# Padding the rows and pools of an encoder-block kernel so that its 512-column matmul operands start at one byte residue

## The chip, the cores and the metric

The kernel runs on one NeuronCore of one Trainium2 chip. The metric is the device time of one execution in microseconds (us), and the number shown for a kernel is the median of its runs. The core has a matrix engine, TensorE (PE in the profile; its weight loads are listed apart as PEld), three engines for element-wise work (VectorE or DVE, ScalarE or ACT, GpSimd or POOL), a queue on SyncE (SP) that issues nearly all DMA transfers, and an on-chip memory, SBUF, of 128 partitions. A tile occupies the same byte addresses in each partition. In this text "the residue" of an operand is its first byte address within a partition modulo 256.

## The reference, cut to what matters

One layer of a hybrid encoder, on 16 learned tokens followed by 1024 rows of `x`, each of 1024 float32 values:

```
u = rms_norm(h) ;  z = u @ w_in                # 1024 -> 7680 columns
A: two-directional retention of 4 heads (128-row chunks), group norm, * silu(gate), @ w_ret_branch
B: attention in a window of +-128 rows, 8 heads in 2 groups, rotary, sink, * silu(gate), @ w_attn_branch
mix = sigmoid(g_A) * A + sigmoid(g_B) * B
out = h + rms_norm(mix @ w_out)                # without the first 16 rows
```

## The kernel before, in words

**Three matmuls for one.** Each float32 product is made from operands split into a high part of type float32r and a low part (the remainder). `mm3` (lines 93 to 98) issues three matmuls into the same PSUM bank: high by high (L95), low by high (L96), high by low (L97). The first argument is stationary (the weights, 128 columns, loaded into the array ahead of the matmul), the second is moving (read column by column, 512 columns in most of the kernel, 256 in the rest).

**Seven products for eight.** The gates, the query projection and the three last projections are computed as 2x2 blocks with seven block products and sums (`Phase`, lines 984 to 1160; `PROD`, line 969). A product is `for k in range(4): mm3(...)`, that is twelve matmuls of 512 columns, on one of seven moving operands: `B11`, `B21`, `T1`, `B22` are parts of `big`; `T2`, `T3`, `T4` are sums of blocks with tiles of their own.

**The moving operands.** `big` (line 153) is four tiles, high and low, of 4 rows of T = 1040 float32 values each, 4160 bytes a row. At first it holds the transposed x (`xh`, `xl`); later phases write the gated results, then `w_out`'s input, into the same tiles. A half of a row starts at column 16 or at column 528 (`half`, line 833). T2 to T4 have rows of 512 values (2048 bytes).

**Where they lie.** Pools are taken from the left end of SBUF upwards or, with `side="right"`, from the right end downwards, each as long as its tiles need. `keep` is the first on the left. In before, the first half-row of `big` starts at byte 6816, residue 160. As 4160 is 16 x 256 + 64, the next rows have residues 224, 32 and 96, and each half-row pair has the same one, since 528 columns are 2112 bytes, 8 x 256 + 64, and 16 columns are 64 bytes. The first phase's T2, T3, T4 (tiles `T2q`, `T3q`, `T4q`, right side) start at 163808, 147424 and 131040: residue 224 in every row. The later T2 to T4 (pool `yt`, left side, above `yp` and `gp`) start at 122720: residue 96 in every row. All weights of 512-column matmuls lie on the right (`wp`, later `lp`) and have residue 224, row by row.

**Stages, in order of time.** (1) Projections of q, k, v of the retention, and the retention (256-column and 512-column matmuls mixed). (2) The keys and values of the attention. (3) The first phase, `first_phase` with names ending in y: two retention gate units and the queries (bank `by`). (4) The attention, with parts of the gate products (`pe`) put between its matmuls. (5) Phase z: the remaining gates (`bz`). (6) Phases r and a: the two branch projections (`br`, `ba`). (7) Phase o: the output (`bo`). Phases 5 to 7 run as one chain of products (`run`, line 1272). The instruction order of each engine comes from a simulated schedule by priorities, made when the program is built.

**Rings.** `stage` (line 978) gives out raw tiles for the next phase's moving operands from two rings: `sg0` in pool `lp` and `sg1` in pool `yp`; each of the four blocks of an operand takes four tiles. `refill` (line 1188) loads them, forms the sums on DVE and splits them into `big` and T2 to T4 as each of those is read for the last time. `gtile` (line 981) gives out tiles of the ring `g`, for gate values (`v`, `tg`), products and scratch. `staged` and `gates_` hold the ring lengths.

```
def stage(name, j=0, dt=F32):
    return (yp if j else lp).tile([P, 512], dt, tag=f"sg{int(j)}", bufs=staged[bool(j)], name=name)
```

Of the kernel before, what the change touches and what calls it, by code (L numbers as in the profile page):

```python
# [7 lines left out]
F32 = mybir.dt.float32  # L8
R = mybir.dt.float32r
# [6 lines left out]
T = NM + SEQ  # L16
P = 128
# [39 lines left out]
def block_kernel(ctx: ExitStack, tc: tile.TileContext, xT, x, meta, w_in, w_rb, w_ab, w_out, vecs, dec, sink,  # L57
# [4 lines left out]
    keep = ctx.enter_context(tc.tile_pool(name="keep", bufs=1))  # L62
# [47 lines left out]
    def dve_lo(o, i, hi):  # L110
        return nc.vector.tensor_tensor(o, i, hi.bitcast(F32), ALU.subtract).ins  # L111
# [38 lines left out]
            split(t, act)  # L150
        return w

    big = [[keep.tile([P, 4, T], R, name=f"big{i}_{s}") for i in range(2)] for s in range(2)]
    xh = [big[0][k // 4][:, k % 4] for k in range(KT)]
    xl = [big[1][k // 4][:, k % 4] for k in range(KT)]

# [362 lines left out]
    z_stack, lp = ExitStack(), None  # L519
# [265 lines left out]
    def part(t, i):  # L785

        return t.rearrange("p a b -> p (a b)")[:, 512 * i:512 * i + 512].rearrange("p (k c) -> p k c", k=4)
# [24 lines left out]
    def pre_split(k, m):  # L812

        n, o, a, b = SUMS[m]
        x = w[k] if m < 3 else w.pop(k)
        nc.vector.tensor_tensor(x[o], x[a], x[b], ALU.subtract)
        if spare[0] is zq:
            h, l = (gtile(f"w{n}{k}{e_}").bitcast(R) for e_ in "hl")
        elif m % 2:
            t = lp.tile([P, 4, 256], F32, tag="w2", bufs=1, name=f"w{n}{k}")  # L820
            h, l = (part(t, e_).rearrange("p k c -> p (k c)").bitcast(R) for e_ in range(2))
        else:
            h, l = (lp.tile([P, 512], F32, tag="c1", bufs=2, name=f"w{n}{k}{e_}").bitcast(R) for e_ in "hl")
        nc.scalar.copy(h, x[o])
        dve_lo(l, x[o], h)
        for t, d in zip((h, l), pre_d[n]):
            nc.sync.dma_start(d[:, k], t.bitcast(F32))

    w, near = {}, []
# [143 lines left out]
    final = "o", 3, 4  # L973
    sub, mul, add = ALU.subtract, ALU.mult, ALU.add

    staged, gates_ = [2, 6], [9]

    def stage(name, j=0, dt=F32):
        return (yp if j else lp).tile([P, 512], dt, tag=f"sg{int(j)}", bufs=staged[bool(j)], name=name)
# [1 line left out]
    def gtile(name):  # L981
        return gp.tile([P, 512], F32, tag="g", bufs=gates_[0], name=name)

    class Phase:
# [116 lines left out]

        def combine(self, u, p, st):
            def new(tag):
                return (lp if tag == "c1" else yp).tile([P, 512], F32, tag=tag, bufs=2, name=f"{tag}{self.nm}{u}")

            def copy(tag):
                st[tag] = new(tag)
                nc.scalar.copy(st[tag], st["X"][0])

            def plus(o, i, at):  # L1110
                near[:] = [nc.vector.tensor_tensor(o, i, st[at][0], add).ins]
                return o

            def done(at):
                free.append(st[at][1])

            apart, early = u in self.apart, u in self.early
            made = {1: (2, 0, 0), 6: (3, 0, 1), 7: (5, 1, 1)}.get(p)
            if made and (u, made[0]) in self.e:
                tag = {1: "c1", 6: "u2", 7: "u3"}[p]  # L1120
                copy(tag)
                e = self.e.pop((u, made[0]))
                nc.vector.tensor_tensor(e, st.pop(tag), e, add)
                self.post(u, *made[1:], e)
            elif p == 1:
                copy("c1")
            elif p == 2:
                self.post(u, 0, 0, plus(st["c1"], st["c1"], "Z"))
                done("Z")
            elif p == 6:  # L1130
                copy("u2")
                if (self.nm, u) == final[:2]:
                    plus(st["u2"], st["u2"], "Y")
                if apart:
                    done("X")
                    st["u3"] = plus(new("u3"), st["u2"], "W")
                if early:
                    plus(st["u2"], st["u2"], "V")
                    done("V")
                    self.post(u, 0, 1, plus(st["u2"], st["u2"], "Y"))  # L1140
            elif p == 7 and not apart:
                copy("u3")
                if (self.nm, u) == final[:2]:
                    done("X")
            elif p == 3 and (self.nm, u) == final[:2]:
                self.post(u, 0, 1, plus(st["u2"], st["u2"], "V"))
                done("V")
            elif p == 3 and not early:
                self.post(u, 0, 1, plus(new("c5") if apart else st["u2"], st["u2"], "Y"))
                done("Y")  # L1150
            elif p == 4 and apart:
                self.post(u, 1, 0, plus(st["u2"], st["u2"], "W"))
                done("W")
            elif p == 4:
                self.post(u, 1, 0, st["X"][0], new("c5"))
                done("X")
            if "u3" in st and "Y" in st and "c22" not in st:
                st["c22"] = plus(new("c5") if (self.nm, u) == final[:2] else st["u3"], st["u3"], "Y")
                self.post(u, 1, 1, st["c22"])
                if early or (self.nm, u) == final[:2]:  # L1160
                    done("Y")
# [549 lines left out]
    def first_weights(u):  # L1711
        for n in ("A11", "A12"):
            first_phase.block(u, n)

    jobs = dict(l=x_load, c=x_scale, s=x_sums, p=x_parts, f=x_first, t=t_store, m=more, n=second_fetch, k=second_parts, x=lambda k: pre_load(k, act_src(w_out)), y=pre_split, A=ready, F=pre_fetch, S=pre_sums, P=pre_parts,
                L=pre_low, z=lambda _: next(first), w=first_weights, r=lambda _: first_phase.raw.clear())

# [17 lines left out]
    yp = gp = spare[0] = zq = zq_stack.enter_context(tc.tile_pool(name="zq", bufs=1, reuse_waits="tile"))  # L1735
# [3 lines left out]
    for n, _ in enumerate(first):  # L1739
# [8 lines left out]
    yp = spare[0] = at1  # L1748
# [19 lines left out]
             46: [(pre_parts, 13)],  # L1768
             47: [(pre_low, 13)],
             48: [(pre_split, 3, 0)],  # L1770
             50: [(pre_split, 3, 1)],
             52: [(pre_split, 3, 2)],
             53: [(pre_sums, 14), (pre_fetch, 15)],
# [5 lines left out]
    i = attention()  # L1779
# [3 lines left out]
    z_stack.close()  # L1783
    w_stack.close()
    free.extend(["p2", "p2"])
    staged[:] = [7, 8]
    lp = ctx.enter_context(tc.tile_pool(name="lp", bufs=1, reuse_waits="tile", side="right"))

    with tc.issue_after(softmax[-3]), tc.issue_after(softmax[-1]):
# [11 lines left out]
    rope_stack.close()  # L1801
    free.extend(["p1", "p1", "p3"])
    yp, gp, yt = (ctx.enter_context(tc.tile_pool(name=n, bufs=1, reuse_waits="tile")) for n in ("yp", "gp", "yt"))
    for n in ("T2", "T3", "T4"):
        B[n] = [yt.tile([P, 4, 512], R, name=f"{n}{s}")[:, :, :] for s in range(2)]
    for n in ("T2", "T3", "T4"):
# [86 lines left out]
```

## Time and profile before

| what | value |
|---|---|
| median of 3 runs | 1047.75 us (1047.32 to 1048.1) |
| the profiled execution's own time | 1047.21 us |
| its span, first to last instruction | 1045.4 us |
| mean granted TensorE clock | 0.996 of full |
| PE busy / DVE busy / ACT busy / POOL busy | 1028.3 / 844.4 / 511.9 / 210.1 us |
| DMA | 217.17 MB, 208 GB/s on average |

Matmuls overlap: one of 512 columns is listed with about 0.39 us, but the next begins 0.23 us after it began. A row "x659" in a view by windows counts the matmuls that touch the window, so the time from one start to the next, called the pitch below, is (window + 0.39) / count. In a timeline it is the difference of two starts, divided by the number of matmuls between them. PE's busy time says nothing about the pitch.

### The profile page before, as it was taken

How to read it: one execution, taken by the hardware profiler on the slowest of the kernel's cores; microseconds unless marked ns; L12 is line 12 of the kernel's file. 1: busy time of each engine (PE TensorE's matmuls, PEld its weight loads, DVE VectorE, ACT ScalarE, POOL GpSimd, SP SyncE). 2: the span in 40 equal slices, each digit the busy share in tenths (PEclk: the TensorE clock that was granted, in tenths of full speed). 3: DMA queues.
4: the chain of work that ended last, by engine and by line, in shares of the span. 5: the costliest groups of instructions: out<-in, count | busy, mean ns of one | idle time of the engine just before them, and what ended most of it. 6: DMA issues, size and time to landing. Idle time of an engine off the chain costs nothing. (4 is left out here: it accounts for less than half of the span.)

```text
span 1045.4 us, 17242 instructions
## 1 busy us (share of the span) xinstructions
PE 1028.3 (98%) x5797; PEld 892.6 (85%) x5797; DVE 844.4 (81%) x1739; ACT 511.9 (49%) x1118; POOL 210.1 (20%) x274
## 2 busy tenths in 40 slices
PE   9999999999999999999899999999999999999997
PEld 8998999989999888888699898888888888787886
DVE  7887788779889787895877886699899799768766
ACT  5641441423435643433677776476567355333432
POOL 4424235235233002331023331000000000111030
PEclk9999999999999999999899999999999999999999
DMA  9322211215244399997976784999889747789472
GB/s 342 156 81 91 82 42 51 72 36 197 77 142 143 120 409 323 267 290 231 325 215 215 240 248 150 361 382 344 301 291 345 243 137 256 207 227 323 108 139 101
DMA packets 117961, 217.17 MB, mean 208 GB/s; under 512 B 12704, under 2 KB 44352, under 8 KB 115280
## 3 DMA queue, kind: packets, MB, share of 16 engines
q1 hardware_dynamic: 112144, 206.09, 57.3%
q0 software_dynamic: 5440, 9.44, 6.1%
q8 instruction: 46, 0.75, 0.3%
q10 hardware_dynamic: 288, 0.53, 0.2%
q14 instruction: 43, 0.35, 0.1%
HBM read 142.57 MB, written 75.55 MB: 209 GB/s over the span
## 5 line engine op out<-in xcount | busy, mean ns | idle before, releaser
L95 PE MATMUL pv<-wh,big 128*128 128x256 f32 x256 | 73.3, 286 | 0.0
L96 PE MATMUL pv<-wh,big 128*128 128x256 f32 x256 | 72.9, 285 | 0.0
L97 PE MATMUL pv<-wl,big 128*128 128x256 f32 x256 | 72.5, 283 | 0.0
L1548 POOL TENSOR_SCALAR p<-p,den 128x352 f32<-128x352 f32 (+2 forms) x56 | 36.3, 661 | 126.2 <-DVE den L1541 53.0
L1371 POOL DMA_DIRECT2D mx_d<-c1a x4 | 3.5, 872 | 287.3 <-DVE c1a L1362 287.3
L95 PE MATMUL bz<-T,lhz 128*128 128x512 f32 x144 | 56.8, 395 | 0.0
L96 PE MATMUL bz<-T,llz 128*128 128x512 f32 x144 | 56.8, 394 | 0.0
L97 PE MATMUL bz<-T,lhz 128*128 128x512 f32 x144 | 56.8, 394 | 0.0
L1014 ACT CAST why<-wry 128x512 fp32r<-128x512 f32 x56 | 33.0, 620 | 47.3 <-PE by L97 26.2
L96 PE MATMUL by<-big,wly 128*128 128x512 f32 x128 | 50.7, 396 | 0.0
L95 PE MATMUL by<-big,why 128*128 128x512 f32 x128 | 50.4, 394 | 0.0
L97 PE MATMUL by<-big,why 128*128 128x512 f32 x128 | 50.4, 393 | 0.0
L96 PEld LDWEIGHTS pv<-wh,big 128*128 128x128 f32 x256 | 48.2, 188 | 0.3
L95 PEld LDWEIGHTS pv<-wh,big 128*128 128x128 f32 x256 | 48.2, 188 | 0.2
L97 PEld LDWEIGHTS pv<-wl,big 128*128 128x128 f32 x256 | 48.3, 189 | 0.2
L1463 POOL DMA_DIRECT2D aq_d<-m_aq x32 | 27.2, 1278 | 104.0 <-DVE u3y L1458 66.1
L111 DVE TENSOR_TENSOR wly<-wry,why 128x512 fp32r<-128x512 f32 x56 | 38.0, 694 | 11.3 <-ACT why L1014 11.2
L1538 ACT ACTIVATE p<-raw,nm 128x353 f32<-128x353 f32 (+2 forms) x64 | 36.2, 567 | 15.5 <-DVE nm L1535 14.6
L596 ACT ACTIVATE op<-pa,rcol 128x256 f32<-128x256 f32 x32 | 15.3, 477 | 41.9 <-PE pa L97 41.6
L658 ACT ACTIVATE ost<-to,rnw 128x128 f32<-128x128 f32 x64 | 20.1, 366 | 31.4 <-PE to L653 21.8
L1535 DVE CUSTOM_DVE_ANT_0 raw<-ps,mask,nsink 128x352 f32<-128x352 f32 (+2 forms) x64 | 33.2, 548 | 2.7 <-ACT p L1538 1.9
L689 POOL TENSOR_TENSOR rs<-rs,mhalf 128x1 f32<-128x1 f32 x32 | 23.3, 727 | 52.5 <-DVE rs L688 49.2
(715 smaller groups left out, 3768.0 us busy)
## 6 DMA issues: line engine op xcount, KB each, us to landing
e<-e SPq DMA_DIRECT2D x60, 256.0 KB, 5.2
we<-in_w_in_dram SPq DMA_DIRECT2D x20, 512.0 KB, 5.5
wr<-in_w_in_dram SPq DMA_DIRECT2D x19, 512.0 KB, 4.2
wry<-in_w_in_dram SPq DMA_DIRECT2D x16, 512.0 KB, 6.9
tg<-tg_d SPq DMA_DIRECT2D x32, 256.0 KB, 5.0
T<-tT SPq DMA_DIRECT2D x6, 1024.0 KB, 10.3
T<-preT SPq DMA_DIRECT2D x6, 1024.0 KB, 7.1
wrz<-in_w_in_dram SPq DMA_DIRECT2D x20, 256.0 KB, 5.3
```

The costliest lines, as they stand in the source:

```text
L95: nc.tensor.matmul(o, ah, bh, start=first, stop=False, **kw)
L96: nc.tensor.matmul(o, al, bh, start=False, stop=False, **kw)
L97: latest[:] = [nc.tensor.matmul(o, ah, bl, start=False, stop=last, **kw).ins]
L111: return nc.vector.tensor_tensor(o, i, hi.bitcast(F32), ALU.subtract).ins
L596: nc.scalar.activation(o, pa[:, 0:256], AF.Copy, scale=rcol[:, c:c + 1])
L658: nc.scalar.activation(ost[0][:, e_, w0:w0 + P], to[:, P * e_:P * e_ + P], AF.Copy, scale=rnw[:, 2 * h + e_:2 * h + e_ + 1])
L689: nc.gpsimd.tensor_tensor(rs, rs, mhalf[:, 0:1], ALU.pow)
L1014: nc.scalar.copy(h, src)
L1463: nc.gpsimd.dma_start(d[a], m2[b], accum_op=ALU.add)
L1535: nc.vector.tensor_tensor_reduce(raw[e_][:, 1:1 + wid], s[:, 0:wid], mask[:, mo:mo + wid], -SCALE, nsink[:, hp:hp + 1], ALU.add, ALU.min, ...
L1538: last["exp"] = nc.scalar.activation(p[:, 0:1 + wid], raw[e_][:, 0:1 + wid], AF.Exp, scale=-1.0, bias=nm_[:, e_:e_ + 1], accum_out=den[:, ...
L1548: nc.gpsimd.tensor_scalar(pt[e_][:, 0:wid], pt[e_][:, 0:wid], den[:, e_:e_ + 1], 1.0, op0=ALU.mult, op1=ALU.mult)
```

## The change

- A tile of 16 float32 columns (64 bytes) is put into `keep` just ahead of `big`.
- The rows of `big` grow from 1040 to 1088 columns, that is from 4160 to 4352 bytes (17 x 256). Only the first 1040 columns are used.
- A tile of 272 columns (1088 bytes, 4 x 256 + 64) is added to pool `gp`, which lies ahead of `yt`.
- The rings are shortened by one tile each: `g` in the first phase from 9 to 8, `sg0` from 7 to 6 and `sg1` from 8 to 7 after the attention.
- The tiles `c1` of the first phase, and those in which `w_out`'s sums are split during the attention, come from `yp` in place of `lp`. Both pools have the same kind of tiles; the right side gets shorter by 4096 bytes for that time.

By the sizes, every half-row of `big` then starts at residue 224: the first at 6880, the rows 4352 bytes apart. `yt` moves up by 64 + 4 x 4 x 192 + 1088 - 2048 = 2176 bytes to 124896, residue 224. The pools on the right move by whole multiples of 2048 bytes, and their residues stay at 224.

```
+    keep.tile([P, 16], F32, name="pad")
-    big = [[keep.tile([P, 4, T], R, name=f"big{i}_{s}") for i in range(2)] for s in range(2)]
+    big = [[keep.tile([P, 4, T + 48], R, name=f"big{i}_{s}")[:, :, 0:T] for i in range(2)] for s in range(2)]
...
-            h, l = (lp.tile([P, 512], F32, tag="c1", bufs=2, name=f"w{n}{k}{e_}").bitcast(R) for e_ in "hl")
+            h, l = (yp.tile([P, 512], F32, tag="c1", bufs=2, name=f"w{n}{k}{e_}").bitcast(R) for e_ in "hl")
...
-    staged, gates_ = [2, 6], [9]
+    staged, gates_ = [2, 6], [8]
...
-                return (lp if tag == "c1" else yp).tile([P, 512], F32, tag=tag, bufs=2, name=f"{tag}{self.nm}{u}")
+                return (lp if tag == "c1" and not self.paired else yp).tile([P, 512], F32, tag=tag, bufs=2, name=f"{tag}{self.nm}{u}")
...
-    staged[:] = [7, 8]
+    staged[:] = [6, 7]
...
+    gp.tile([P, 272], F32, name="pad")
```

## The prediction

> **What bounds the kernel now.** I read the page first, then PE's waits, then busy time by stage.
>
> ```profile
> span 1045.4 us, 17242 instructions
> PE 1028.3 (98%) x5797; PEld 892.6 (85%) x5797; DVE 844.4 (81%) x1739; ACT 511.9 (49%) x1118; POOL 210.1 (20%) x274
> ```
> ```profile
> PE pt L1559 <- ACT p L1545: 2.7, 1, 2.7
> PE ps L95 <- DVE nm L1535: 2.4, 1, 2.4
> ```
> ```profile
> core 0: us, PE busy (x) PEld busy (x) DVE busy (x) ACT busy (x) POOL busy (x), PEclk, DMA share, GB/s
> 335.00:505.00 170.00, 170.00 (x749) 138.58 (x749) 135.51 (x226) 73.46 (x133) 30.54 (x36) 1.00 0.86 271
> 505.00:530.00 25.00, 19.93 (x99) 16.68 (x98) 19.47 (x49) 16.93 (x42) 2.61 (x5) 0.86 0.77 265
> 650.00:806.00 156.00, 155.71 (x678) 126.19 (x677) 136.79 (x224) 93.51 (x171) 0.00 (x0) 1.00 0.96 340
> 806.00:873.00 67.00, 67.00 (x290) 54.30 (x289) 57.47 (x94) 33.88 (x62) 0.00 (x0) 1.00 0.58 188
> 873.00:958.00 85.00, 85.00 (x366) 68.46 (x365) 64.55 (x106) 32.34 (x56) 8.70 (x10) 1.00 0.84 250
> 958.00:1046.00 88.00, 79.80 (x355) 64.68 (x353) 61.42 (x113) 34.80 (x74) 14.47 (x18) 0.98 0.53 144
> ```
>
> TensorE is the bound from end to end. Its two longest waits, at the start of the attention, come to 5.1 us, and in the first phase (335 to 505) and phases z to o (from 650) it is never idle for more than a moment. No engine there is waited for; DVE, at 88% in phase z, is the next. So only two things can change the time: the rate at which PE gets through matmuls that are all ready, or a new wait.
>
> That rate is the pitch, the time from one matmul's start to the next one's. The view by windows gives its mean, over stretches that hold almost only 512-column matmuls:
>
> ```profile
> 350.00:500.00 150.00, 150.00 (x654) 1.00 0.91 285
> 664.00:806.00 142.00, 142.00 (x613) 1.00 0.97 342
> 806.00:884.00 78.00, 78.00 (x338) 1.00 0.63 206
> 894.00:958.00 64.00, 64.00 (x277) 1.00 0.81 232
> 964.00:1026.00 62.00, 62.00 (x268) 1.00 0.55 126
> ```
>
> First phase: 150.39 / 654 = 230.0 ns. The other four together: 347.6 / 1496 = 232.3 ns. The clock is granted in full, so 2 ns between stages is not the clock. PE's timeline, product by product (twelve matmuls from the first row of a pair to the second), shows what differs:
>
> ```profile
> 392.39 0.39 PE L95 MATMUL by<-T2q,why 128*128 128x512 f32 x1
> ...
> 395.16 0.39 PE L95 MATMUL by<-T2q,why 128*128 128x512 f32 x1
> ...
> 397.88 0.39 PE L95 MATMUL by<-big,why 128*128 128x512 f32 x1
> ```
> ```profile
> 674.59 0.39 PE L95 MATMUL bz<-T,lhz 128*128 128x512 f32 x1
> ...
> 677.38 0.39 PE L95 MATMUL bz<-T,lhz 128*128 128x512 f32 x1
> ...
> 844.68 0.39 PE L95 MATMUL br<-big,lhr 128*128 128x512 f32 x1
> ...
> 847.46 0.39 PE L95 MATMUL br<-big,lhr 128*128 128x512 f32 x1
> ```
>
> The first product on T2q, just behind one on big, takes 2.77 us (230.8 ns a matmul), the second 2.72 (226.7); the later T takes 2.79 (232.5), big 2.78 (231.7). Same width, same engine, no waits. By the layout, T2q and its weights both have residue 224; the later T has residue 96 against weights at 224; the rows of big go through 160, 224, 32 and 96. So the trace holds one measured case in which moving operand and weights share a residue, and there the pitch settles, after some matmuls, at 226.7 ns. The rows of big leave no time to settle, since each is read by three matmuls only. Higher address bits don't seem to matter: rows of big an odd multiple of 256 apart (its two high tiles lie 16640 bytes from each other) show the same pitch as rows 2048 apart.
>
> **The change part by part.**
>
> *Residues.* After it every 512-column moving operand has residue 224 and meets weights at 224, the case of T2q. Nothing then changes between products, so I take 226.7 ns for all of them. Phases z to o: PE is busy 155.7 + 67.0 + 85.0 + 79.8 = 387.5 us; times (1 - 226.7 / 232.3) that is **9.4 us**. First phase: 170.0 x (1 - 226.7 / 230.0) = **2.4 us**. There are also some 470 512-column matmuls in the retention's projections and between the attention's matmuls, in runs of 3 to 24 among other widths; at the full 5.6 ns they would give 2.6 us, but a run of 3 to 12 is over before the pitch has settled: I take **1.0 us**, with 0 and 2.6 as ends. From below: if the shared residue never gave more than the mean of the first phase, 230.0, phases z to o would gain 387.5 x 2.3 / 232.3 = 3.8 us and the first phase nothing.
>
> [...]
>
> *256-column matmuls.* The projections for v have x as the stationary operand. The first 16 columns of x are in a small tile of their own (`xm`), with residue 224 on both sides; two runs on it bound the cost, and a run of 24 on big lies between them:
>
> ```profile
> 241.48 0.28 PE L181 MATMUL pv<-wl,xm 128*16 128x256 f32 x1
> ...
> 243.28 0.28 PE L95 MATMUL pv<-wh,big 128*128 128x256 f32 x1
> ```
> ```profile
> 309.99 0.28 PE L95 MATMUL pav<-wh,big 128*128 128x256 f32 x1
> ...
> 312.83 0.28 PE L95 MATMUL pav<-wh,big 128*128 128x256 f32 x1
> ...
> 320.06 0.28 PE L179 MATMUL pav<-wh,xm 128*48 128x256 f32 x1
> ...
> 321.88 0.28 PE L95 MATMUL pav<-wh,big 128*128 128x256 f32 x1
> ```
>
> On `xm`, 15 matmuls in 1.80 us are 120 ns each, and 16 in 1.82 us are 113.8. With one residue, then, 256 columns settle at one of several pitches; on big 24 take 2.84 us, 118.3. About 1470 such matmuls: between 1470 x 1.7 ns = 2.5 us lost and 1470 x 4.5 ns = 6.6 us gained; I take **0**, since the middle of the two ends, 116.9, is the nearest to today's, and nothing says which of them comes.
>
> *Pads, and c1 in another pool.* No instruction is added: the padded columns are never read or written, the operands' shapes are the same, and no DMA has other bytes. The c1 tiles keep their count of two. Cost 0; no other work covers it, as there is none.
>
> *Rings.* The loads of the next phase's blocks run ahead as far as the ring goes. In phases z and r sg1 has to hold eight live tiles (two blocks of four), and now has seven. The eighth load must wait until the first of the others has been split for the last time, which is when T2 (at the end of z) or T3 (at the end of r) comes free. For z:
>
> ```profile
> 790.14 2.18 ACT L1664 CAST T<-z 128x512 fp32r<-128x512 f32 x4
> ```
> ```profile
> 814.03 0.39 PE L95 MATMUL br<-T,lhr 128*128 128x512 f32 x1
> ```
> ```profile
> z<-oTr_d SPq DMA_DIRECT2D x16, 256.0 KB, 5.4
> ```
>
> Today T2's four rows are cast from 790.14 and first read at 814.03. With seven tiles the fourth row's load starts when the first has been cast and its low part made, about 792; it lands 5.4 us later, about 797.5; two DVE sums, a cast and a low part (0.7 us each, DVE is busy) bring it to 801 to 804. Read at 815, so 10 us are left: hidden under the eight products between. At the end of r the products come in the same order, and T3 comes free two products after T2, so some 5 us less are left. Behind that load on SP stand the next weights, and PE waits for those only once six prepared products are used up, some 16 us. In the first phase one tile fewer in ring g delays a load of gate values by at most the time of one product pair; PE has no wait there to make longer. I take **0.5 us** lost for all rings, with 0 and 5.4 (one landing in the open) as ends; nothing can be won, since PE isn't idle.
>
> *Sum.* 1047.2 (profiled execution) - 9.4 - 2.4 - 1.0 + 0.5 = 1034.9. The median of the runs is 0.5 above that execution, so **1035.4 us**. Late afterwards is still PE: DVE rises from 88% to 90% of phase z. DMA there already carries 340 GB/s at 0.96 of its time and must do the same bytes in 2.4% less.
>
> **The rivals.**
>
> *B, part of it.* The pitch settles less well, because casts and sums disturb it or the 256-column runs settle on 120, or the DMA of phase z and the shorter rings take some microseconds back. For it: DMA's 0.97 in the row for 664 to 806. Against it: T2q settled with DMA at 0.86 over the whole phase. Half of 12.8 us is left: 1047.75 - 6.4 = 1041.3, from 1038 to 1044.
>
> *C, it doesn't do what it says.* The 226.7 ns belongs to T2q's place high in SBUF or to the first phase, not to the residue. Then PE's time stays: 1047.5. For it: only the tiles of one phase show it. Against it: in that same phase T2q itself needs a product to settle when it comes behind big, as a state would that the operands' sequence makes, and a place would not. [...]
>
> *D, slower: the eighth load is late.* SP works in order, and some of its waits are long:
>
> ```profile
> SPq L1293 <- DVE str3S L1042: 13.3, 1, 13.3
> ```
> ```profile
> 867.84 0.33 SPq L1307 DMA_DIRECT2D r<-oTa_d  x1
> ```
> ```profile
> 515.70:521.20 5.50, 5.50 (x19) 0.51 0.99 376
> ```
>
> If the load of T2's fourth row stands behind one such wait, it is ready at 803 + 13.3 = 816, about when it is read; that is the point from which it decides. Behind two it is 14 us late, PE stands still, and as after the attention's start (waits of 2.4 and 2.7 us, then 5.5 us at clock 0.51) about 2.7 us more go at half clock. Loss 16.7 us against the gain of 12.8: 1047.75 + 16.7 - 12.8 = 1051.6. For it: the ring is really too short by one. Against it: the build's schedule knows the ring and places the load on SP accordingly, and today's eighth load of sg0 at the end of r, which has seven tiles already and goes out at 867.84, long after its fellows, costs PE nothing.
>
> **How the numbers follow.** Forecast 64%, B 18%, C 7%, D 11%. About 0.2%, 2.1 us, is what a measurement of this kernel can tell from no change. Faster by more: forecast and B, 82%, and 1% of C; within: 6% of C and 1% of D; slower: 10%. The range: the forecast's low end takes 2.6 instead of 1.0 and some of the 256-column gain, 1032; upward it takes in B to 1044. It leaves out C, D and the edges, about 20%.
>
> **What the profile after would show.** If right: the four late windows give 226 to 228 ns by the same sum, big and T alike; a product takes 2.72 us; PE has no new wait above 1 us. If B: some windows at 228 to 230, or new waits of PE on casts fed by z or r loads. If C: 232 as before. If D: a wait of PE on T's cast near 810 or 890 and a clock below 1.00 after it. The forecast is wrong if the pitch of T2q doesn't carry over to big.

## The result, and the profile after

The changed kernel takes 1039.12 us (median of 6 runs, 1035.18 to 1041.84) against 1047.92 us (6 runs, 1046.56 to 1048.3): a ratio of 0.9914, 95% interval 0.9898 to 0.9931. It is 8.8 us faster where 12.4 were foretold, inside the range. Twelve later runs gave 0.9926 (0.9904 to 0.9948).

The page of the changed kernel, its first line and the row of busy times:

```profile
span 1035.8 us, 17254 instructions
...
PE 1018.4 (98%) x5797; PEld 893.7 (86%) x5797; DVE 841.5 (81%) x1739; ACT 512.5 (49%) x1118; POOL 210.4 (20%) x274
```

The same 5797 matmuls; PE is busy 9.9 us less, and the span is 9.6 us shorter. Where that lies is seen by windows (PE alone: window, busy time and count of matmuls, PEclk, DMA share, GB/s), again in stretches that hold almost only 512-column matmuls:

```profile
350.00:495.00 145.00, 145.00 (x643) 1.00 0.92 287
664.00:800.00 136.00, 136.00 (x601) 1.00 0.97 339
830.00:880.00 50.00, 50.00 (x222) 1.00 0.59 193
890.00:940.00 50.00, 50.00 (x223) 1.00 0.84 234
965.00:1020.00 55.00, 55.00 (x245) 1.00 0.47 108
```

By (window + 0.39) / count the pitch is 226.1, 226.9, 227.0, 226.0 and 226.1 ns, where before had 230.0 and then 232.3. (One matmul more or less at an edge is 0.4 to 1 ns in these rows.) The timeline shows it without that rounding, over an edge from big to T:

```profile
683.76 0.39 PE L95 MATMUL bz<-big,lhz 128*128 128x512 f32 x1
...
685.80 0.39 PE L95 MATMUL bz<-T,lhz 128*128 128x512 f32 x1
...
688.52 0.39 PE L95 MATMUL bz<-T,lhz 128*128 128x512 f32 x1
```

Nine matmuls on big in 2.04 us and twelve on T in 2.72 are both 226.7 ns: no product has to settle any more.

What the prediction did not have is in the waits (engine, tile, line <- what released it: us in all, times, longest) and in the 256-column projections. The lines of the program are one further down than in before:

```profile
PE pt L1560 <- ACT p L1546: 2.3, 1, 2.3
...
PE bo L95 <- ACT lho L1015: 1.4, 2, 1.1
PE pe L96 <- DVE w_4l L111: 1.3, 1, 1.3
PE ps L95 <- DVE nm L1536: 0.9, 1, 0.9
```
```profile
247.98 0.28 PE L95 MATMUL pv<-wh,big 128*128 128x256 f32 x1
...
249.78 0.28 PE L95 MATMUL pv<-wh,big 128*128 128x256 f32 x1
```

The wait on w_4l is new; it comes where the parts of the gate products fill in ahead of the attention. The wait of ps fell from 2.4 to 0.9, so that the two together are no longer than before, 2.2 us against 2.4. And on big fifteen 256-column matmuls take 1.80 us, 120 ns each, where the run of 24 quoted in the prediction took 118.3.

### The profile page after: what moved, and what is told of

Same layout as the page of the kernel before. It is cut to its first block, busy times and chain, and to the rows that moved or that the text cites. A ratio compares the mean times of both kernels' runs of the same rounds, so it can differ in the third digit from the quotient of the medians.

```text
span 1035.8 us, 17254 instructions
## 1 busy us (share of the span) xinstructions
PE 1018.4 (98%) x5797; PEld 893.7 (86%) x5797; DVE 841.5 (81%) x1739; ACT 512.5 (49%) x1118; POOL 210.4 (20%) x274
```

## Theories and experiments

**Theory E, equal residues.** The pitch of matmuls that follow one another without waits depends on the difference of the residues of moving and stationary operand, and at 512 columns it is shortest when that is 0. **Rivals:** the gain comes from the rings or from c1's new place; from the residue 224 itself; from all moving operands being alike, whatever the weights have. Below, "difference" is moving minus stationary residue, modulo 256. The "settled pitch" is the mean of the last six starts-to-starts of a product of twelve, and the time of a bank is the sum of the starts-to-starts of its matmuls, both from the start times in the trace. Edits are against the changed kernel.

### The rings and c1 alone

```
-    keep.tile([P, 16], F32, name="pad")
-    big = ... keep.tile([P, 4, T + 48], R, ...)[:, :, 0:T] ...
+    big = ... keep.tile([P, 4, T], R, ...) ...
...
-    gp.tile([P, 272], F32, name="pad")
```

> The rings shortened and c1 moved as in the change, without any pad: big goes through residues 160, 224, 32, 96 and the late T lies at 96, as before. Theory (the gain is the pitch of 512-column matmuls alone, the rings cost a little): pitch of the four late stages 232.3 ns as before, and 0.5 to 2.5 us slower than before, 1048.3 to 1050.3. Rival (the rings or the new order that comes with them carry part of the gain): faster than before by 1 us or more.

1049.16 us (10 runs, 1044.97 to 1055.8) against 1048.41 on that chip: ratio 1.0013 (0.9993 to 1.0034). By windows the late stages are as before, 136.39 / 590 = 231.2 and 60.39 / 260 = 232.3 ns, and from start to start 232.0 to 232.3 in all four banks:

```profile
664.00:800.00 136.00, 136.00 (x590) 1.00 0.95 330
...
890.00:950.00 60.00, 60.00 (x260) 1.00 0.83 239
```
```profile
PE pe L96 <- DVE w_4l L111: 3.1, 1, 3.1
```

So the gain is not the rings'. The wait on w_4l doesn't need the pads: it is here without any, 3.1 us long, and before has none. That the rings or c1 make it is likely, but not shown: it stands in every profile of a kernel with the shorter rings, from 0.5 to 5.2 us, except that of the next run, whose rings are the same. It doesn't show as a loss that the interval could tell from nothing.

### Uniform, but not equal

```
-    keep.tile([P, 16], F32, name="pad")
```

Without the first pad big and the late T2 to T4 all start at 160, and the weights stay at 224.

> The change without its 64-byte pad ahead of big: every 512-column moving operand of big and of the late T has residue 160, all weights stay at 224. Theory E (moving operand and weights must have the same residue): late pitch 230 to 233.5 ns, time that of before plus the rings, 1047 to 1051; only the first phase's T2q to T4q products stay at 226.7. Rival U (it is enough that all moving operands have one residue, so that nothing changes between products): late pitch 226.7, time as with the change, 1036 to 1042.

1048.35 us (10 runs, 1046.21 to 1052.01): ratio 1.0002 (0.9985 to 1.0019). The whole gain is gone, although all moving operands of the late phases are alike. The timeline, over big, T and big again:

```profile
704.18 0.39 PE L95 MATMUL bz<-big,lhz 128*128 128x512 f32 x1
...
706.98 0.39 PE L95 MATMUL bz<-T,lhz 128*128 128x512 f32 x1
...
709.78 0.39 PE L95 MATMUL bz<-T,lhz 128*128 128x512 f32 x1
...
712.58 0.39 PE L95 MATMUL bz<-big,lhz 128*128 128x512 f32 x1
```

Each product of twelve takes 2.80 us: it locks at 233.3 ns as firmly as the changed kernel does at 226.7, and 1 ns above the unsettled 232.3 of before. Uniformity fixes the pitch; which pitch, the difference says.

### Everything at 96

```
-    keep.tile([P, 16], F32, name="pad")
+    keep.tile([P, 48], F32, name="pad")
...
+    wp.tile([P, 32], F32, name="padw")
...
-    staged[:] = [6, 7]
+    staged[:] = [6, 6]
...
+    lp.tile([P, 32], F32, name="padl")
```

> The changed kernel with everything 128 bytes further: every 512-column moving operand at residue 96 and every weight of them at 96 too (sg1 one tile shorter still, to make room). Theory E (equality of the two residues is what counts): pitch 226.7 in the stages by to bo, time that of the change, 1037 to 1042. Rival A (residue 224 itself is the good place): pitch 230 to 233, 1046 to 1051.

1036.65 us (5 runs, 1033.36 to 1041.22) against 1046.4 there: ratio 0.9919 (0.9893 to 0.9944), 0.3 us below the expected range. By windows:

```profile
664.00:800.00 136.00, 136.00 (x601) 1.00 0.96 331
802.00:870.00 68.00, 68.00 (x302) 1.00 0.68 232
```

136.39 / 601 = 226.9 and 68.39 / 302 = 226.5 ns, and every settled product is at 226.7. The residue 224 is nothing special; being equal is.

### The late T2 to T4 alone, and big alone

Late T at 224 and rows of 4160 bytes as before:

```
-    keep.tile([P, 16], F32, name="pad")
-    big = ... keep.tile([P, 4, T + 48], R, ...)[:, :, 0:T] ...
+    big = ... keep.tile([P, 4, T], R, ...) ...
...
-    gp.tile([P, 272], F32, name="pad")
+    gp.tile([P, 32], F32, name="pad")
```

> Only the late T2 to T4 are moved to residue 224 (a pad of 128 bytes ahead of them); big keeps its rows of 4160 bytes; rings as in the change. Theory E: products on the late T at 226.7 to 229 ns (somewhat above 226.7 just behind a product on big), on big at 232; T has somewhat under half of the 1644 late matmuls, so about 3 to 4 us gained and 1 to 2 lost by the rings: 1044.5 to 1046.5. Rival U: no stage settles while big changes its residue, late pitch 232, 1048 to 1050.

Big at 224, and the late T at 96 as before:

```
-    gp.tile([P, 272], F32, name="pad")
+    gp.tile([P, 240], F32, name="pad")
```

> Big's rows at residue 224 as in the changed kernel, but the late T2 to T4 at 96 again, as before; weights at 224. Theory (the pitch follows the difference of the residues, and a product needs some matmuls to come to its own pitch): the first phase as in the changed kernel (152.7 us for its bank); in phases z to o the products on big end near 227 ns, those on T near 232, the stages at 229.5 to 230.5, and the time is 1042 to 1044, the mirror of the run with the late T alone. Rival (the gain comes only if no operand breaks the sequence): big stays above 230 as well, stages 231.5 to 232.5, time 1045 to 1046.

T alone: 1043.5 us (10 runs, 1042.06 to 1048.7), 0.9958 (0.9938 to 0.9978), 1 us below the expected range. Big alone: 1043.79 (6 runs, 1041.48 to 1046.48), 0.9954 (0.993 to 0.9977). The same two windows of the run with T alone, then of that with big alone:

```profile
664.00:800.00 136.00, 136.00 (x595) 1.00 0.96 335
...
890.00:950.00 60.00, 60.00 (x262) 1.00 0.83 235
```
```profile
664.00:800.00 136.00, 136.00 (x589) 1.00 0.96 338
...
890.00:950.00 60.00, 60.00 (x262) 1.00 0.83 236
```

229.2 and 230.5 ns with T, 231.6 and 230.5 with big. By the times each part has about half of the gain (0.0042 and 0.0046 of 1, where the changed kernel has 0.0086 and 0.0074), but with intervals of 0.002 to either side they can't tell whether the parts add up. The banks tell more. Against before, bz, br, ba and bo together are 1.0 us shorter with T alone (3.1 without the two late matmuls of br, behind a wait of 1.8 us on u3r), 2.6 shorter with big alone, and 7.8 with both; big alone has 2.7 more from the first phase. In the late phases both together thus give more than the sum of the two.

The settled pitches fit that. Big alone settles at 226.7 behind its T at 233.2. With T alone, a product on T behind one on big comes to 228.8 and only a second on T to 226.7 (227.8 over all), while big's rows of 4160 bytes stay at 232.6. So the rival that one odd operand spoils the whole sequence falls, but a product needs five matmuls (big behind T) to ten (T behind big) to come to its own pitch, and that is what an edge costs. Phase z with big alone, at 231.6, was over its expected 230.5; the three other stages and the time lay within.

### Six other differences

T2, T3 and T4 of the late phases 32, 64 and 96 bytes past the weights in one run, 160, 192 and 224 past them in another, big and the weights at 224 (the second with 40, 8 and 8 columns):

```
-    gp.tile([P, 272], F32, name="pad")
+    gp.tile([P, 16], F32, name="pad")
     for n in ("T2", "T3", "T4"):
+        yt.tile([P, {"T2": 8, "T3": 8, "T4": 8}[n]], F32, name=f"sp{n}")
```

> The changed kernel with the late T2 at residue 0, T3 at 32, T4 at 64, that is 32, 64 and 96 bytes above their weights (224, modulo 256); big stays at 224. Theory E: T2, T3, T4 each settle at some other pitch than 226.7, between 228 and 236, big at 226.7 in the middle of its products. An open question: whether one of these differences gives a shorter pitch than 226.7. Rival U would have 226.7 for all within a product.

> As before it, with the late T2 at 128, T3 at 160, T4 at 192: 160, 192 and 224 bytes above their weights. By uniform_160, T3 settles at 233.3 ns (its operands and weights are as far apart there). T2 and T4: between 228 and 236; whether one is shorter than 226.7 is open.

One run each, 1045.1 and 1039.62 us, which say little by themselves. What was wanted are the settled pitches, means over 20 to 22 products of each tile:

| difference | 0 | 32 | 64 | 96 | 128 | 160 | 192 | 224 |
|---|---|---|---|---|---|---|---|---|
| ns | 226.7 | 233.4 | 228.9 | 233.8 | 232.1 to 233.2 | 234.2 | 233.3 | 233.3 |

(0 is the changed kernel's, 128 the late T of before and of big alone; before's don't settle on one value.) Two products of the first scan's timeline, T3 (708.10 to 710.86, 230 ns with its settling) and T2 (722.04 to 724.84, 233.3 ns):

```profile
708.10 0.40 PE L95 MATMUL bz<-T,lhz 128*128 128x512 f32 x1
...
710.86 0.39 PE L95 MATMUL bz<-T,lhz 128*128 128x512 f32 x1
...
722.04 0.40 PE L95 MATMUL bz<-T,lhz 128*128 128x512 f32 x1
...
724.84 0.40 PE L95 MATMUL bz<-T,lhz 128*128 128x512 f32 x1
```

No step of 32 bytes is better than equality, 64 is next, and the place within 256 bytes that before's operands happened to have costs 5 to 6 ns in 227.

### The changed kernel again

No edit.

> The changed kernel once more, for a second profile and more times. Its six times spread over 6.7 us, those of before over 1.7. Theory S (with equal residues, runs of 256-column matmuls settle at 113.3, 116.7 or 120 ns as it happens, and the clock's half-rate stretch at the start varies): the stages by to bo take the same sum as in the first profile, 528.3 us, within 1 us, and the difference between the two profiles' spans lies in the first 335 us and the attention. Rival R (the shorter rings sometimes make PE wait): the difference lies in waits of PE in the stages z to o.

1039.82 us (12 runs, 1036.3 to 1046.46), 0.9926 (0.9904 to 0.9948). The banks by to bo take 528.0 us where the first profile had 528.3, as expected. The 256-column projections stand at the same means as in the first profile, to 0.1 ns (v 119.3, k 119.0 to 119.1): they don't settle as it happens, as theory S had it, and are not some accident of a run. The wait on w_4l is there again, and longer:

```profile
PE pe L96 <- DVE w_4l L111: 2.7, 1, 2.7
```

### The weights up to the attention moved: 256 columns

If the difference decides at 256 columns too, 0 is the wrong one there. A pad in `wp` of 16 columns (8 and 48 in the other two runs) moves the weights of the projections and of the first phase, and T2q to T4q with them, away from big; `wp` ends before the late phases, which stay as they are.

```
     k_stack.close()
+    wp.tile([P, 16], F32, name="padw")
     z_stack.close()
```

> The changed kernel with all weights up to the attention (and the first phase's T2 to T4 beside them) 64 bytes lower, at residue 160; big at 224, everything after the attention as in the changed kernel. 256-column projections: the difference is now 64 instead of 0. Theory: their pitch too goes by the difference of the residues, 0 is the bad one at 256 columns (120 ns), and they come to 116 to 117.5 (about 1390 matmuls x 2 to 3 ns = 3 to 4 us less); the first phase pays about 1 us, since big against its weights then settles at 228.9 and T2q at 226.7; time 1036 to 1038, 2 us below the changed kernel. Rival: the 256-column matmuls stay at 119 to 120 wherever the weights lie; then only the first phase's loss is left, and the time is 1040 to 1041.

> As the last, with 32 bytes instead of 64: weights up to the attention at 192, big at 224. Theory: 512-column matmuls on big settle at 233.3 against these weights, so the first phase's bank takes 154.5 to 156 us (152.7 in the changed kernel); 256-column matmuls, with a difference of 32, differ from 119.3 in one direction or the other; no time is foretold to better than 1037 to 1042. Rival: both as in the changed kernel, 152.7 us and 119.3 ns.

> As the last, with 192 bytes: weights up to the attention at 32, big at 224, the same difference as in the run with everything but the weights at 160. Theory (only the difference counts): projections of k at 116.5 ns and of v at 117.4, as there, about 3 us less than in the changed kernel; the first phase's products on big end at 233.3 and its bank takes 154.5 to 156 us, 2 to 3 us more; time 1038.5 to 1041, about as the changed kernel. Rival (the place counts, not the difference): the 256-column matmuls stay at 119.3.

With 64 bytes: 1035.83 us (5 runs, 1033.8 to 1043.61) against 1048.49 there, ratio 0.99 (0.9868 to 0.9931). That is just below the expected 1036, but the interval overlaps that of the changed kernel, 0.9904 to 0.9948 in its later runs, so the times don't tell the two apart. With 32 and 192 bytes one run each, 1040.89 and 1039.76. The projections for v in the run with 64 bytes:

```profile
243.31 0.28 PE L95 MATMUL pv<-wh,big 128*128 128x256 f32 x1
...
247.39 0.28 PE L95 MATMUL pv<-wh,big 128*128 128x256 f32 x1
```

36 matmuls in 4.08 us are 113.3 ns each, against 120 above. The means over all 256-column matmuls on big, those without a wait, and the first phase's bank:

| kernel | weights | v of the retention | its k | v of the attention | its k | first phase, us |
|---|---|---|---|---|---|---|
| before | 224, big mixed | 118.1 | 118.0 | 118.4 | 118.1 | 155.36 |
| changed | 224, big 224 | 119.3 | 119.0 | 119.7 | 119.3 | 152.69 |
| 64 bytes | 160, big 224 | 115.9 | 117.3 | 117.2 | 117.7 | 154.24 |
| 32 bytes | 192, big 224 | 118.3 | 117.1 | 118.3 | 117.6 | 155.65 |
| 192 bytes | 32, big 224 | 117.2 | 116.8 | 115.7 | 115.9 | 155.45 |
| uniform | 224, big 160 | 117.4 | 116.3 | 117.5 | 116.3 | 155.45 |

The weights are the moving operand for v and the stationary one for k, so each row has one difference for v and its opposite for k: with 64 bytes 192 and 64, with 32 bytes 224 and 32, with 192 bytes and in the uniform kernel 64 and 192.

As the theory has it, every other difference that was tried (32, 64, 192, 224) is better than 0 for 256 columns, and none is for 512 (the first phase is slower in all four than in the changed kernel). Weights at 32 with big at 224 and weights at 224 with big at 160 have one difference, and their pitches are alike within 0.6 ns but for v of the attention (1.8): that speaks for the difference and not the place, though at 256 columns something else counts too (in the last run below, with the residues of the one with 64 bytes, the same v takes 116.3 ns in place of 117.2). With 64 bytes the sum is 768 x 3.4 + 288 x 1.7 + 192 x 2.5 + 144 x 1.6 ns = 3.8 us won, 1.55 lost in the first phase.

The first phase is the clearest test at 512 columns, since only the weights (and T2q to T4q with them) move there and big stays at 224. Two products on big, with 64 bytes and then with 192:

```profile
397.28 0.39 PE L95 MATMUL by<-big,why 128*128 128x512 f32 x1
...
400.02 0.40 PE L95 MATMUL by<-T3q,why 128*128 128x512 f32 x1
```
```profile
411.93 0.39 PE L95 MATMUL by<-big,why 128*128 128x512 f32 x1
...
414.73 0.39 PE L95 MATMUL by<-big,why 128*128 128x512 f32 x1
```

They take 2.74 and 2.80 us. The settled pitch, a mean over 17 products on big, is 226.7 ns in the changed kernel and 228.9, 233.3 and 233.4 with the differences 64, 32 and 192: what the late T had at the same differences, within 0.1 ns.

### The ring one tile shorter still

In five profiles PE comes late a few times in banks br and ba: the two of the changed kernel and the three with the weights moved, all with the late operands at one residue and with a ring sg1 of 7 tiles. The banks' time less 336 x 226.67 ns is 0.3 and 1.0 us in the first profile of the changed kernel, 1.3 and 1.2 with the weights 64 bytes lower, and up to 2.2 and 1.4 in the others; in the run at 96, whose sg1 has 6 tiles, it is nothing. (The 2.1 and 1.8, 0.7 and 1.6 us of the expectation below are the same late matmuls with their own pitch counted in.) The last kernel has the 64 bytes and

```
-    staged[:] = [6, 7]
+    staged[:] = [6, 6]
```

> The last of these versions: the weights up to the attention at residue 160 and everything else of 512 columns at 224, as in the run that gave 1035.8 us, and ring sg1 after the attention one tile shorter still (6 and 6, the lengths of the run with everything at 96). Theory: the late matmuls of banks br and ba (2.1 and 1.8 us over their pitch in that run, 0.7 and 1.6 in the changed kernel, none in the run at 96) come from the order that goes with the ring of 7, not from its place; with 6 they go, bz, br, ba and bo stay at 226.7 to 226.8 ns, and the time is 1032 to 1035. Rival: they come with the residues' place or with the run, and a shorter ring only brings loads later: banks br and ba keep 1 us or more of late matmuls each, or T's casts are waited for at 800 to 810 us, and the time is 1035 to 1039.

1036.9 us (6 runs, 1033.81 to 1039.67) against 1049.22 there: ratio 0.9885 (0.986 to 0.9909). Bank br took 76.16 us, which is 336 x 226.67 to the last digit, and of ba's 0.8 us over it all lies at its end, in the wait for the next phase. With the run at 96, two profiles with 6 tiles have no late matmul in br, nor in ba before its end, and five with 7 have them, so at 226.7 ns those waits come with the ring of 7, as supposed. (At longer pitches a ring of 7 alone doesn't make them: br has none with the rings alone and in the uniform kernel.) The time was not as expected, though: 1036.9 is above 1032 to 1035 and in the rival's range. This profile's start of phase o tells why one profile is a poor judge of 2 us (windows as above):

```profile
948.00:951.00 3.00, 1.81 (x7) 1.00 1.04 400
951.00:955.00 4.00, 3.46 (x8) 0.59 1.04 419
```

PE idles for 1.2 of 3 us there, for the weights of phase o, and then eight matmuls take 427 ns each, in 4 us at a granted clock of 0.59: 1.6 us lost. By ratio this version is ahead of the changed kernel's 0.9914 by 0.003, but the intervals overlap, and the profile doesn't show a gain either: the banks by to bo take 531.0 us against the changed kernel's 528.3, with 1.5 more in the first phase and those 1.6 in phase o, and what the 256-column matmuls give, some 3.9 us by their means, doesn't show in the span, 1036.5 us at a mean clock of 0.994 against 1035.8 at 0.997. Whether it is faster than the changed kernel stays open.

Not tried: the retention's weights alone moved by 64 bytes, with the first phase's left at 224, which would keep both gains.

## Why the prediction was right, and where it was off

*The residues.* Right in mechanism and size. The 1644 matmuls of banks bz, br, ba and bo went from 232.3 to 226.7 or 226.8 ns: 9.2 us, where 9.4 were foretold (its own product gives 9.3). What came back is new waits in them: their sum fell by 7.8 us (3.65, 1.57, 1.16 and 1.40), so 1.4 us of the gain went into waits that the prediction had put at none of above 1 us, ba's 1.0 being at that limit. The first phase's bank gave 2.7 (foretold 2.4).

*The runs of 3 to 24 among others.* Foretold 1.0. The queries came to 228.8 ns from 232.0 (192 matmuls, 0.6 us) and the gate products in the attention to 230.3 from 232.3 (some 320 without a wait, 0.6 us): 1.2 us, and, as supposed, most are over before they settle.

*256 columns.* This is the term that was mis-sized: taken as 0, with ends of 2.5 lost and 6.6 won, it is 768 x 1.2 + 288 x 1.0 + 192 x 1.3 + 144 x 1.2 ns = 1.6 us lost (0.2 come back in the 272-column matmuls, 125.6 to 124.1 ns). The step that failed is "I take 0, since the middle of the two ends, 116.9, is the nearest to today's, and nothing says which of them comes". The reason doesn't give that number: 116.9 is 1.4 ns below 118.3, which is 2.1 us gained over 1470 matmuls. That the 0 came out nearer than its own reason is luck. On big, with 1392 such matmuls, difference 0 settles on 120 (means of 119.0 to 119.7); the run on `xm` at 113.8 stays unexplained.

*Rings.* Foretold 0.5 lost, 0 to 5.4. The run with the rings alone gives 1.4 lost, from 0.7 won to 3.6 lost: no more than that can be said. The loads of T, rival D, were not late: no wait of PE on T's casts shows. The wait that did come is elsewhere, on w_4l ahead of the attention, and was not in the prediction. With 7 tiles in sg1 come the waits of banks br and ba too, which the prediction didn't have.

*The sum.* 9.2 - 1.4 + 2.7 + 1.2 - 1.4 = 10.3 us against 9.6 between the two profiled executions. The rest is in the attention, where waits on w_4l and ps came and went, and in five late matmuls of the queries (four of them at 427 ns, between 7.2 and 9.8 us; 1.2 us over their pitch in that profile, 0.1 in the one of before). Some luck is in it too: at the attention's start before lost 5.5 x (1 - 0.51) = 2.7 us to the clock and the changed kernel 7 x (1 - 0.76) = 1.7 (its row stands in the last section), and the next profile of the changed kernel was at 0.89 from 500 to 530 us, like before, where its first was at 0.94. That the change shortens the stretch at a lower clock is not shown. Of the signs that the prediction named, the windows at 226 to 228 and the product of 2.72 us came; "no new wait above 1 us" failed by the 1.3 us on w_4l, and the longest wait of bo grew from 0.8 to 1.1. Then the median: the prediction put it 0.5 above the profiled execution, and it is 1.5 above (1039.12 against 1037.57). With 256 columns (1.4) and the waits (1.4, less the 0.5 foretold for the rings) that is nearly all of the 3.7 between 1035.4 and 1039.12.

*The rivals.* C is excluded by the windows and D by the waits. B's time, 1038 to 1044, is the one that came. Of the causes that it named, 256 columns on 120 is shown, the shorter rings are likely (but the interval of their run alone includes zero), and the pitch of the 512-column matmuls settled as the forecast had it: forecast and B are both partly true.

## What to carry to other kernels

This was seen on one kernel, whose matmuls are all of float32r parts, each with a weight load ahead of it (5797 of either on the page). Where matmuls follow one another without waits, compare the pitch of tiles that differ in nothing but their address; a stretch that is faster than its neighbours shows what the layout could be. Then lay out weights and moving operands by the difference of their residues for the width that most matmuls have (here 512 columns, 226.7 ns with equal residues), look at the other widths for what they lose (here 256 columns, with means on big of 119.0 to 119.7 ns at difference 0 and 115.7 to 118.3 at the others), and give rows a pitch that keeps the residue. Change all operands together: with half of them moved, the late phases had less than half of the gain (1.0 and 2.6 us of 7.8). A gain spread over a thousand small steps is judged by sums over all of them and by runs in number, not by one profile.

## What was not expected of the hardware

- **The pitch went with address differences.** It is from 226.7 to 234.2 ns at 512 columns and from 113.3 to 120 at 256 columns, at a granted clock of 1.00, and the best difference of one width is the worst of those tried for the other. Two kernels that differ only in a pad of 64 bytes ahead of `big`, the changed one and the uniform one, settle at 226.7 and 233.3 ns. Why, these runs don't show.
- **One difference can have two settled pitches.** In the run with big at 160 the projections for k ran at 113.3 ns (first two rows, 15 matmuls in 1.70 us), and a few us later the same code on the same residues at 117.9 (last two, 33 in 3.89 us):

```profile
298.98 0.28 PE L95 MATMUL pak<-big,wh 128*128 128x256 f32 x1
...
300.68 0.28 PE L95 MATMUL pak<-big,wh 128*128 128x256 f32 x1
...
302.42 0.28 PE L95 MATMUL pak<-big,wh 128*128 128x256 f32 x1
...
306.31 0.28 PE L95 MATMUL pak<-big,wh 128*128 128x256 f32 x1
```

- **Stretches at a granted clock of 0.50 make about half of the spread, by an estimate from the mean clocks.** The changed kernel's 12 further runs go from 1036.3 us at a mean clock of 0.997 to 1046.46 at 0.992; those 0.005 are 5 us of the 10. Around the attention's start, where PE waits, the granted clock from 500 to 530 us was 0.89 in before and in the second profile of the changed kernel, 0.94 in its first and 0.83 with big alone, and from 200 to 330 us it was 1.00 in all four. In the last 2 us, where PE has no matmul left, before and the changed kernel have 0.50. By windows, the changed kernel, where before was at 0.51 from 515.7 to 521.2:

```profile
514.00:521.00 7.00, 7.00 (x33) 0.76 1.00 393
```
